# The gate third of adaLN: from PSUM sums beside the output projection to SBUF sums beside the latent projections, with part of the weight split on GpSimd

## The chip, the cores and the metric

The kernel runs on one core of one Trainium2 chip. The metric is the device time of one execution in microseconds (us). The median of three runs before the change is 2997.7 us.

## What is computed

One layer of a latent-token block with D = 4096, 256 latent tokens and 256 context tokens, all in float32. The reference, cut to what matters here:

```python
mod = jax.nn.silu(c) @ w_ada + b_ada                  # (4096) @ (4096, 12288)
shift, scale, gate = jnp.split(mod, 3, axis=-1)
h = modulate(rmsnorm(x, g_norm), shift[:, None], scale[:, None])
proj = h @ w_in                                       # 4096 -> 16384, latent tokens
xa, xb, ga, gb = jnp.split(proj, [LRU_W, MIX_W, MIX_W + LRU_W], axis=-1)
...                                                   # xa also for the context tokens
ya, ya_c = rglru_branch(xa, xa_c, ...)                # two gated linear recurrences, 16 heads
yb = pool_branch(xb, w_pool, b_pool, pool_scale)
mixed = jnp.concatenate([ya * silu(ga), yb * silu(gb)], axis=-1)
x_new = x + gate[:, None] * (mixed @ w_out)           # 8192 -> 4096
return rmsnorm(x_new, g_final)
```

The change is about `gate`, the last third of `mod`: a matrix of 4096 x 4096 multiplied with one vector. It is needed first where the first block of the output projection is finished.

## The kernel before, in words

Tokens lie along the free axis, features along the 128 partitions. Every large weight comes from HBM in tiles of 128 x 1024 float32 (512 KB). A product with such a weight is made in two parts: ScalarE rounds the raw tile to `hi` (L97), another engine subtracts to get `lo = raw - hi` (L99), and TensorE multiplies with both (L566 with `hi`, L567 with `lo`). This is `load_w`. There are 6 buffers for raw tiles, 4 for `hi` and 3 for `lo`. So the `lo` of one weight unit can be written as soon as the unit three places earlier is used up.

The program has three stages on TensorE. First the adaLN columns for shift and scale and the projection `xa`, in nine chunks of the contraction (L237, L337 to L339); here GpSimd makes the `lo` tiles, and VectorE sums adaLN weights into PSUM (`wide`, L213) and finishes each chunk's activations (`hlo`, L131). Then the latent projections: 384 tiles of `w_lat` and 32 of `w_pool`, with the 32 tiles of `w_rec` and the recurrent branch spread among them; here VectorE makes every `lo` tile. Last the output projection, 256 tiles of `w_out`, again with every `lo` on VectorE.

The gate third is cut into four groups of 1024 columns. For each, `gate_units` loads 32 raw tiles, and VectorE adds each, times one element of the vector per partition, to a PSUM accumulator: `accumulate`, L213, with the last step written as two halves `fin` (L219). Two matmuls with a column of ones (L279), a copy and eight small records of transposing matmuls (L192) turn the 1024 sums over partitions into columns of `gate` (L288). Group 0 stands near the end of the latent projections (`GATE_FROM, GATE_END` = 0.9, 0.99 of that list), groups 1 to 3 among the output projection's units (`GATE3`). Its raw tiles share the 6 raw buffers.

The code writes one list of events: `w` units with a weight split, `a` units with a raw tile only, `s` steps. `run` walks it and starts loads a few units ahead. A scheduler of the framework then settles the order of each engine's own queue. Each engine works through its queue in that order. SP's queue issues all the loads.

Of the kernel before, what the change touches and what calls it, by code (L numbers as in the profile page):

```python
# [7 lines left out]
F32 = mybir.dt.float32  # L8
# [3 lines left out]
ADD, SUB, MUL = ALU.add, ALU.subtract, ALU.mult  # L12
# [6 lines left out]
HEADS = 16  # L19
KEEP = 8  # L20
DELAY = 8
GATE3 = (0.08, 0.7)
GATE_FROM, GATE_END = 0.9, 0.99
SPILL_Y = 10
EPS = 1e-6
POOL_ADDS = 3
# [20 lines left out]


def spread(main, side, lo=0.0, hi=1.0):
    """Places the entries of side evenly among those of main, from the fraction lo of main to hi."""  # L50
    out, done, n = [], 0, len(main)
    a, b = lo * n, hi * n
    for i, m in enumerate(main):
        out.append(m)
        want = min(len(side), max(0, int((i + 1 - a) / (b - a) * len(side) + 1e-9)))
        while done < want:
            out.append(side[done])
            done += 1
    return out + side[done:]
# [3 lines left out]
def block_kernel(ctx, tc, xc, cvec, vecs, consts, w_ss, w_gate, w_xa, w_lat, w_pool, w_rec, w_out, out):  # L63
# [7 lines left out]
    rawp = ctx.enter_context(tc.tile_pool(name="raw", bufs=RAWB))  # L71
    hip = ctx.enter_context(tc.tile_pool(name="hi", bufs=HIB))
    lop = ctx.enter_context(tc.tile_pool(name="lo", bufs=LOB))
    ps_mm = ctx.enter_context(tc.tile_pool(name="ps_mm", bufs=4, space=bass.MemoryType.PSUM))
    ps_2 = ctx.enter_context(tc.tile_pool(name="ps_2", bufs=2, space=bass.MemoryType.PSUM))

# [6 lines left out]
    def mm_tile():  # L83
        return ps_mm.tile([P, 512], F32, name="mm", tag="mm")

    def wide_tile():
        return ps_2.tile([P, 1024], F32, name="wide", tag="wide")

    def load_raw(src):
        t = rawp.tile([P, W], F32, name="raw", tag="raw")  # L90
        nc.sync.dma_start(out=t, in_=src)
        return t

    def load_w(src, eng=None):
        raw = load_raw(src)
        hi = hip.tile([P, W], F32R, name="hi", tag="hi")
        act.copy(out=hi, in_=raw)  # L97
        lo = lop.tile([P, W], F32R, name="lo", tag="lo")
        (eng or dve).tensor_tensor(out=lo, in0=raw, in1=hi.bitcast(F32), op=SUB)  # L99
        return hi, lo  # L100

    def run(events):
        queues = {}
        for kind, look in (("w", LOOK), ("a", LOOK_A)):
            queues[kind] = [[e for e in events if e[0] == kind], [], 0, look]
        for e in events:
# [16 lines left out]
    def A_(src, f):  # L123
        return ("a", src, f)

    def S_(f):
        return ("s", f)
# [2 lines left out]
        act.copy(out=hi, in_=src)  # L130
        dve.tensor_tensor(out=lo, in0=src, in1=hi.bitcast(F32), op=SUB)  # L131

# [1 line left out]
    cst = cpool.tile([P, 276], F32, name="cst")  # L134
    nc.sync.dma_start(out=cst, in_=consts)
    ident = cst[:, 0:4]
# [12 lines left out]
    def vrange(name, a, b):  # L149
        o = _VEC[name][0]  # L150
        return vec[:, o + a:o + b]
# [6 lines left out]
    act.activation(out=sig, in_=sig, func=AF.Sqrt)  # L158

    def rstd_of(ps, r, v, s):  # L160
        """Leaves -2 * rsqrt(ps / D + EPS) in r: one Newton step after the square root."""
        dve.tensor_scalar(out=v, in0=ps, scalar1=1.0 / D, scalar2=EPS, op0=MUL, op1=ADD)
        act.activation(out=s, in_=v, func=AF.Sqrt)
        dve.reciprocal(out=r, in_=s)
        dve.tensor_tensor(out=v, in0=v, in1=r, op=MUL)
        dve.tensor_tensor(out=v, in0=v, in1=r, op=MUL)
        dve.scalar_tensor_tensor(out=r, in0=v, scalar=-3.0, in1=r, op0=ADD, op1=MUL)

# [1 line left out]
    colA = cpool.tile([P, KT, 2], F32, name="colA")  # L170
    colB = cpool.tile([P, KT, 2], F32, name="colB")
    gate = cpool.tile([P, KT], F32, name="gate")
# [10 lines left out]
    def take_rows(rows_ps, nv, width):  # L183
        rb = temp("rows")
        act.copy(out=rb[0:nv, :width], in_=rows_ps[0:nv, :width])
        return rb

    def to_cols(rb, nv, width, dst):
        cols = mm_tile()
        nb = width // P  # L190
        for b in range(nb):
            pe.matmul(out=cols[:, nv * b:nv * b + nv], lhsT=rb[0:nv, b * P:(b + 1) * P], rhs=ident[0:nv, 0:nv],  # L192
                      start=True, stop=True)
        dst(cols[:, 0:nv * nb].rearrange("p (b v) -> p b v", v=nv))
# [70 lines left out]
    def gate_units(grp):  # L265
        st = {}

        def unit(k):
            def f(raw):
                if k == 0:  # L270
                    st["accs"] = [wide_tile()]
                    st["fin"] = {}
                accumulate(raw, 0, W, k, st["accs"], 1, 512, st["fin"], k == 0, k == KT - 1)
            return A_(w_gate[grp, k], f)

        def rows():
            r = mm_tile()
            for h in range(2):
                pe.matmul(out=r[0:2, :], lhsT=sel[:, h, 0:2], rhs=st["fin"][h, 0], start=(h == 0), stop=(h == 1))  # L279
            st["rb"] = take_rows(r, 2, 512)  # L280

        def cols():
            o = grp * 8

            def dst(cols):
                g = gate[:, o:o + 8].rearrange("p (h b) -> p b h", h=2)
                bias = vrange("b_ada", 64 + o, 64 + o + 8).rearrange("p (h b) -> p b h", h=2)
                dve.tensor_tensor(out=g, in0=cols, in1=bias, op=ADD)  # L288
            to_cols(st["rb"], 2, 512, dst)
        return [unit(k) for k in range(KT)], S_(rows), S_(cols)  # L290

# [1 line left out]
    hT = [None] * KT  # L293
    hc = [None] * KT

# [20 lines left out]
            hc[k] = None  # L316
        return S_(f)

# [1 line left out]
    acc = [None] * 32  # L320
    xa_sp = [None] * (2 * KEEP) + [dram.tile([P, 512], F32, name=f"xa_sp{o}") for o in range(2 * KEEP, 32)]
    ya_sp = [dram.tile([P, 512], F32, name=f"ya_sp{h}") for h in range(HEADS)]
# [56 lines left out]

    ada = [ada_units(c) for c in range(NC)] + [([],)]  # L380

# [1 line left out]
    xt = []  # L383
    first = ada[0][0] + list(ada[0][1:])

# [50 lines left out]
        if c == 1:  # L436
            events.append(S_(softplus))

# [1 line left out]
    def lru_pieces(h):  # L440
        st = {}

# [94 lines left out]
            return [sigm(d, 0), sigm(d, 1), expo(d), root(d), scan(d, 0), scan(d, 1)]  # L537
        return [conv(0), conv(1)], [gates(0)] + post(0) + [gates(1)], post(1)

# [1 line left out]
    def fold(ps, dst):  # L541
        tmp = temp("fold")
        act.copy(out=tmp[:, 0:T], in_=ps[:, T:T2])
# [118 lines left out]
    events.append(S_(make_pads))  # L662
    events += rec[:2]
    both = spread(main, rec[2:], 0.0, LRU_SPAN / 100)
    gu, gr, gc = gate_units(0)
    both = spread(both, gu, GATE_FROM, GATE_END)
    events += both[:-4] + [gr] + both[-4:-1] + [gc] + both[-1:]

# [1 line left out]
    mix = [None] * 64  # L670

    def make_mix(n):
# [43 lines left out]
    main = [block_units([w_out[blk, i] for i in range(16)], mix, out_evac(blk)) for blk in range(16)]  # L716
    pair = [u for two in zip(main[0], main[1]) for u in two]
    main = spread(pair, [make_mix(n) for n in range(4, 32)], 0.0, 28 / 32) + [u for m in main[2:] for u in m]
    side, held = [], []
    for grp in range(1, 4):  # L720
        gu, gr, gc = gate_units(grp)
        side += gu[:2] + held[:1] + gu[2:4] + held[1:] + gu[4:]
        held = [gr, gc]
    side += held
    events += spread(main, side, GATE3[0], GATE3[1])

    run(events)

# [88 lines left out]
```

## Time and profile before

| | |
|---|---|
| runs | 2989.14, 2997.7, 2999.48 us; median 2997.7 us |
| profiled execution | span 2998.8 us from the first to the last instruction (the page gives no other time of it) |
| TensorE | busy 2909.6 us, 97% of the span |
| VectorE | busy 2256.7 us, 75% |
| ScalarE | busy 1559.9 us, 52% |
| GpSimd | busy 530.7 us, 18% |

The profile names the engines PE (TensorE matmul), PEld (TensorE weight load), DVE (VectorE), ACT (ScalarE), POOL (GpSimd) and SP. L99 is line 99 of the kernel. A busy time is the time in which at least one instruction of the engine was under way. Idle time matters only on the engine that sets the end of a stage.

### The profile page before, as it was taken

Reading aid. Unit: us, or ns where it says so; the run is one execution under the profiler, and the core shown is the slowest. Engines: PE = TensorE matmul, PEld = TensorE weight load, DVE = VectorE, ACT = ScalarE, POOL = GpSimd, SP = SyncE. Lnnn points to the kernel's source line nnn. Section 1 sums busy time; section 2 is a strip of 40 time slices with the busy share of each in tenths; the row PEclk is TensorE's granted clock in tenths of the full one; section 3 lists DMA queues with packets and bytes.
Section 4 is the critical chain, followed back from the end, with each engine's and each line's share of the span. In section 5 each row is a group of like instructions: output and inputs, shape, how many; then the busy total and the mean of one; then the engine's idle time right before and its main releaser. Section 6 shows DMA issues by size and latency. Waiting matters only on the chain.

```text
span 2998.8 us, 40342 instructions
## 1 busy us (share of the span) xinstructions
PE 2909.6 (97%) x14992; PEld 2405.3 (80%) x14992; DVE 2256.7 (75%) x2661; ACT 1559.9 (52%) x2112; POOL 530.7 (18%) x304
## 2 busy tenths in 40 slices
PE   5999999999999999999999999999999999999997
PEld 2656777778788888888888888888888888878886
DVE  6999999998447788888777777778888766665444
ACT  4442344434436666677666666666464443333442
POOL 1466777777520000000000000000000000000000
PEclk9999999999999999999999999999999999999998
DMA  8777787887365555565665566667978888786665
GB/s 301 279 261 252 262 263 261 272 277 250 126 183 176 176 177 175 179 183 172 186 185 181 185 188 189 196 195 251 326 232 318 318 288 286 264 279 216 193 191 171
DMA packets 201142, 679.47 MB, mean 227 GB/s; under 512 B 22000, under 2 KB 30320, under 8 KB 200944
## 3 DMA queue, kind: packets, MB, share of 16 engines
q1 hardware_dynamic: 200944, 676.89, 68.9%
q8 instruction: 117, 1.92, 0.3%
q14 instruction: 81, 0.66, 0.1%
HBM read 661.60 MB, written 15.20 MB: 226 GB/s over the span
## 4 chain that ended last, share of the span: by engine, by line
PE 84%; DVE 6%; DMA 6%; issue 1%; POOL 1%; ACT 1%; SPq 0%; DVEq 0%; POOLq 0%; ACTq 0%
PE mm L566 38%; PE mm L567 19%; PE mm L337 6%; PE mm L338 6%; PE mm L339 6%; DMA raw<-in_w_gate 4%; DVE wide L213 3%; PE wide L478 2%; PE wide L480 2%; PE wide L479 2%; PE mm L237 2%; DMA raw<-in_w_ss 1%; DMA x<-in_xc 1%; DVE lo L99 1%; DVE hlo L131 1%
## 5 line engine op out<-in xcount | busy, mean ns | idle before, releaser
L97 ACT CAST hi<-raw 128x1024 fp32r<-128x1024 f32 x832 | 871.9, 1049 | 968.6 <-PE mm L566 576.3
L99 DVE TENSOR_TENSOR lo<-raw,hi 128x1024 fp32r<-128x1024 f32 x704 | 856.5, 1221 | 371.5 <-PE mm L567 282.7
L566 PE MATMUL mm<-hT,hi 128*128 128x512 f32 x3072 | 1086.8, 399 | 0.0
L567 PE MATMUL mm<-hT,lo 128*128 128x256 f32 x3072 | 862.7, 281 | 0.0
L213 DVE SCALAR_TENSOR_TENSOR wide<-raw,sc,wide 128x1024 f32<-128x1024 f32 (+1 forms) x556 | 662.4, 1240 | 153.5 <-DMA raw<-in_w_gate 119.6
L566 PE MATMUL mm<-mix,hi 128*128 128x512 f32 x2048 | 724.7, 398 | 0.0
L566 PEld LDWEIGHTS mm<-hT,hi 128*128 128x128 f32 x3072 | 577.2, 188 | 144.5 <-ACT mix L130 0.9
L567 PE MATMUL mm<-mix,lo 128*128 128x256 f32 x2048 | 577.4, 282 | 15.3 <-DVE lo L99 15.1
L567 PEld LDWEIGHTS mm<-hT,lo 128*128 128x128 f32 x3072 | 580.2, 189 | 1.3
L566 PEld LDWEIGHTS mm<-mix,hi 128*128 128x128 f32 x2048 | 386.0, 188 | 95.1 <-ACT hi L97 1.7
L337 PE MATMUL mm<-hhi,hi 128*128 128x512 f32 x1024 | 404.1, 396 | 13.1 <-ACT hhi L130 10.7
L338 PE MATMUL mm<-hlo,hi 128*128 128x512 f32 x1024 | 402.1, 393 | 9.0 <-DVE hlo L131 9.0
L567 PEld LDWEIGHTS mm<-mix,lo 128*128 128x128 f32 x2048 | 388.2, 190 | 20.8 <-DVE lo L99 20.5
L339 PE MATMUL mm<-hhi,lo 128*128 128x512 f32 x1024 | 401.0, 392 | 0.0
L99 POOL TENSOR_TENSOR lo<-raw,hi 128x1024 fp32r<-128x1024 f32 x128 | 310.6, 2427 | 207.5 <-PE mm L339 87.8
L337 PEld LDWEIGHTS mm<-hhi,hi 128*128 128x128 f32 x1024 | 193.4, 189 | 73.0 <-ACT hhi L130 11.8
L346 POOL TENSOR_TENSOR acc<-acc,part 128x512 f32<-128x512 f32 x168 | 221.7, 1331 | 116.8 <-ACT part L345 115.8
L338 PEld LDWEIGHTS mm<-hlo,hi 128*128 128x128 f32 x1024 | 193.6, 189 | 53.3 <-DVE hlo L131 13.4
L339 PEld LDWEIGHTS mm<-hhi,lo 128*128 128x128 f32 x1024 | 193.6, 189 | 42.2 <-issue 1.7
L345 ACT COPY part<-mm 128x512 f32<-128x512 f32 x168 | 97.3, 584 | 155.4 <-PE mm L339 155.0
L348 DVE TENSOR_TENSOR acc<-mm,acc 128x512 f32<-128x512 f32 x88 | 60.1, 685 | 56.6 <-PE mm L339 56.5
L478 PE MATMUL wide<-uhi,hi 128*128 128x512 f32 x256 | 100.5, 393 | 0.0
(134 smaller groups left out, 2203.0 us busy)
## 6 DMA issues: line engine op xcount, KB each, us to landing
raw<-in_w_lat SPq DMA_DIRECT2D x384, 512.0 KB, 3.7
raw<-in_w_ss SPq DMA_DIRECT2D x256, 512.0 KB, 4.6
raw<-in_w_out SPq DMA_DIRECT2D x256, 512.0 KB, 4.6
raw<-in_w_xa SPq DMA_DIRECT2D x128, 512.0 KB, 4.4
raw<-in_w_gate SPq DMA_DIRECT2D x128, 512.0 KB, 4.8
raw<-in_w_rec SPq DMA_DIRECT2D x32, 512.0 KB, 3.6
raw<-in_w_pool SPq DMA_DIRECT2D x32, 512.0 KB, 3.7
x<-in_xc SPq DMA_DIRECT2D x32, 256.0 KB, 6.6
```

The source lines that it names most:

```text
L97: act.copy(out=hi, in_=raw)
L99: (eng or dve).tensor_tensor(out=lo, in0=raw, in1=hi.bitcast(F32), op=SUB)
L213: dve.scalar_tensor_tensor(out=accs[v][:, :width], in0=seg, scalar=s, in1=accs[v][:, :width], op0=MUL, op1=ADD)
L337: pe.matmul(out=ps, lhsT=wh, rhs=a, start=(k == 0), stop=False)
L338: pe.matmul(out=ps, lhsT=wh, rhs=b, start=False, stop=False)
L339: pe.matmul(out=ps, lhsT=wl, rhs=a, start=False, stop=(k == n - 1))
L345: act.copy(out=part, in_=ps)
L346: nc.gpsimd.tensor_tensor(out=acc[o], in0=acc[o], in1=part, op=ADD)
L348: dve.tensor_tensor(out=acc[o], in0=ps, in1=acc[o], op=ADD)
L478: pe.matmul(out=o, lhsT=wh[:, g, k, m], rhs=st["hi"][k], start=(k == 0), stop=False)
L566: pe.matmul(out=ps, lhsT=hi[:, k, m], rhs=a, start=first, stop=False)
L567: pe.matmul(out=ps[:, 0:T], lhsT=lo[:, k, m], rhs=a[:, 0:T], start=False, stop=last)
```

## The change

All four groups of the gate third move to the latent projections, spread over the fractions 0.02 to 0.94 of that list. Each weight tile goes to a buffer of a pool of its own (`graw`, two buffers), loaded one ahead. The accumulator is one SBUF tile (`gacc`, one buffer) and no longer a PSUM tile. The sum over partitions is made by eight matmuls that take 128 columns of the accumulator as weights and one column of ones as the moving operand. And of the entries of the latent list every third, where it is a weight unit, gets its `lo` tile from GpSimd: 150 tiles of the 448. The output projection's list holds weights alone. The program is also built with a smaller scratch space for DMA descriptors.

```diff
-GATE3 = (0.08, 0.7)
-GATE_FROM, GATE_END = 0.9, 0.99
+GATE_FROM, GATE_END = 0.02, 0.94
+POOL_LO = 3
+LOOK_G = 1
...
+    graw = ctx.enter_context(tc.tile_pool(name="graw", bufs=1 + LOOK_G))
+    gaccp = ctx.enter_context(tc.tile_pool(name="gacc", bufs=1))
...
+    def load_gate(src):
+        t = graw.tile([P, W], F32, name="graw", tag="graw")
         nc.sync.dma_start(out=t, in_=src)
         return t
...
-        for kind, look in (("w", LOOK), ("a", LOOK_A)):
+        for kind, look in (("w", LOOK), ("a", LOOK_A), ("g", LOOK_G)):
...
-            for kind in ("w", "a"):
+            for kind in ("w", "a", "g"):
...
         def unit(k):
             def f(raw):
+                s = sc6[:, k, 2:3]
                 if k == 0:
-                    st["accs"] = [wide_tile()]
-                    st["fin"] = {}
-                accumulate(raw, 0, W, k, st["accs"], 1, 512, st["fin"], k == 0, k == KT - 1)
-            return A_(w_gate[grp, k], f)
-
-        def rows():
-            r = mm_tile()
-            for h in range(2):
-                pe.matmul(out=r[0:2, :], lhsT=sel[:, h, 0:2], rhs=st["fin"][h, 0], start=(h == 0), stop=(h == 1))
-            st["rb"] = take_rows(r, 2, 512)
+                    st["acc"] = gaccp.tile([P, W], F32, name="gacc", tag="gacc")
+                    dve.tensor_scalar(out=st["acc"], in0=raw, scalar1=s, scalar2=None, op0=MUL)
+                else:
+                    dve.scalar_tensor_tensor(out=st["acc"], in0=raw, scalar=s, in1=st["acc"], op0=MUL, op1=ADD)
+            return ("g", w_gate[grp, k], f)
 
         def cols():
+            c = mm_tile()
+            for b in range(8):
+                pe.matmul(out=c[:, b:b + 1], lhsT=st["acc"][:, b * P:(b + 1) * P], rhs=ones[:, 0:1],
+                          start=True, stop=True)
             o = grp * 8
...
+            dve.tensor_tensor(out=gate[:, o:o + 8], in0=c[:, 0:8], in1=vrange("b_ada", 64 + o, 72 + o), op=ADD)
+        return [unit(k) for k in range(KT)] + [S_(cols)]
...
-    gu, gr, gc = gate_units(0)
-    both = spread(both, gu, GATE_FROM, GATE_END)
-    events += both[:-4] + [gr] + both[-4:-1] + [gc] + both[-1:]
+    gates = [u for grp in range(4) for u in gate_units(grp)]
+    both = [e[:3] + (nc.gpsimd,) if e[0] == "w" and i % POOL_LO == 0 else e for i, e in enumerate(both)]
+    events += spread(both, gates, GATE_FROM, GATE_END)
...
-    for grp in range(1, 4):
-        gu, gr, gc = gate_units(grp)
-        side += gu[:2] + held[:1] + gu[2:4] + held[1:] + gu[4:]
-        held = [gr, gc]
-    side += held
-    events += spread(main, side, GATE3[0], GATE3[1])
+    events += main
...
-    nc = bacc.Bacc("TRN2", target_bir_lowering=False, num_devices=1)
+    nc = bacc.Bacc("TRN2", target_bir_lowering=False, num_devices=1, dynamic_dma_scratch_size=1024)
```

The scheduler decides where the gate steps end up in the queues. They are not spread evenly. A group has one accumulator, which is free again only when the matmuls of the group before have read it. All 32 steps of the first group stand in VectorE's queue ahead of the first `lo` of the latent projections, 20 of them behind the last long run of adaLN sums (`wide`) of the first stage. The other three groups follow each in one crowd. Between the first and the last step of a group stand 41, 36 and 40 weight units, of which GpSimd makes 14, 11 and 13 `lo` tiles. Between the crowds there is no gate step for 59 and 62 units, and none for the last 96.

VectorE's queue in the latent projections of the kernel before, at the convolution of a head (`u`, `ulo`), between two pooling steps:

```order
L459 SCALAR_TENSOR_TENSOR u_11052<-acc_673,vec_85,u_11052 128x2x255
L99 TENSOR_TENSOR lo_10926<-raw_10922,hi_10924 128x1024
L459 SCALAR_TENSOR_TENSOR u_11052<-acc_673,vec_85,u_11052 128x2x255
L459 SCALAR_TENSOR_TENSOR u_11052<-acc_673,vec_85,u_11052 128x2x254
L99 TENSOR_TENSOR lo_10948<-raw_10944,hi_10946 128x1024
L131 TENSOR_TENSOR ulo_11058<-u_11052,uhi_11057 128x512
L99 TENSOR_TENSOR lo_10980<-raw_10976,hi_10978 128x1024
L99 TENSOR_TENSOR lo_11012<-raw_11008,hi_11010 128x1024
```

The same place in the changed kernel, in the second gate group's crowd (`gacc` is the accumulator, `graw` a gate tile):

```order
L462 SCALAR_TENSOR_TENSOR u_11200<-acc_681,vec_91,u_11200 128x2x255
L107 TENSOR_TENSOR lo_11068<-raw_11064,hi_11066 128x1024
L462 SCALAR_TENSOR_TENSOR u_11200<-acc_681,vec_91,u_11200 128x2x255
L283 SCALAR_TENSOR_TENSOR gacc_10183<-graw_12465,sc6_96,gacc_10183 128x1024
L462 SCALAR_TENSOR_TENSOR u_11200<-acc_681,vec_91,u_11200 128x2x254
L283 SCALAR_TENSOR_TENSOR gacc_10183<-graw_12556,sc6_96,gacc_10183 128x1024
L139 TENSOR_TENSOR ulo_11206<-u_11200,uhi_11205 128x512
L107 TENSOR_TENSOR lo_11125<-raw_11121,hi_11123 128x1024
L283 SCALAR_TENSOR_TENSOR gacc_10183<-graw_12663,sc6_96,gacc_10183 128x1024
L283 SCALAR_TENSOR_TENSOR gacc_10183<-graw_12744,sc6_96,gacc_10183 128x1024
L107 TENSOR_TENSOR lo_11179<-raw_11175,hi_11177 128x1024
```

Four gate steps stand among three `lo` tiles; the `lo` tiles that are missing in this list are on GpSimd's queue, one behind the other.

VectorE's queue in the first stage of the kernel before, at the end of the second to last chunk, where the next chunk's columns (`colB`, `colA`) and activations (`hlo`) are made:

```order
L219 SCALAR_TENSOR_TENSOR fin_6070<-raw_6018,sc6_90,wide_5182 128x512
L348 TENSOR_TENSOR acc_884<-mm_6048,acc_884 128x512
L202 TENSOR_TENSOR colB_95<-mm_6117,vec_85 128x8
L203 TENSOR_TENSOR colA_94<-mm_6117,vec_85 128x8
L204 TENSOR_TENSOR colA_94<-colA_94,vec_85 128x8
L131 TENSOR_TENSOR hlo_6129<-x_329,hhi_6128 128x512
L131 TENSOR_TENSOR hlo_6172<-x_334,hhi_6171 128x512
```

The same place in the changed kernel:

```order
L227 SCALAR_TENSOR_TENSOR fin_6074<-raw_6026,sc6_96,wide_5190 128x512
L351 TENSOR_TENSOR acc_892<-mm_6054,acc_892 128x512
L283 SCALAR_TENSOR_TENSOR gacc_7150<-graw_8331,sc6_96,gacc_7150 128x1024
L283 SCALAR_TENSOR_TENSOR gacc_7150<-graw_8439,sc6_96,gacc_7150 128x1024
L283 SCALAR_TENSOR_TENSOR gacc_7150<-graw_8518,sc6_96,gacc_7150 128x1024
L283 SCALAR_TENSOR_TENSOR gacc_7150<-graw_8599,sc6_96,gacc_7150 128x1024
L210 TENSOR_TENSOR colB_101<-mm_6121,vec_91 128x8
L211 TENSOR_TENSOR colA_100<-mm_6121,vec_91 128x8
L212 TENSOR_TENSOR colA_100<-colA_100,vec_91 128x8
L283 SCALAR_TENSOR_TENSOR gacc_7150<-graw_8678,sc6_96,gacc_7150 128x1024
L139 TENSOR_TENSOR hlo_6133<-x_335,hhi_6132 128x512
L283 SCALAR_TENSOR_TENSOR gacc_7150<-graw_8789,sc6_96,gacc_7150 128x1024
```

Steps of the first gate group stand ahead of the columns and between the activations of the last chunk.

## Rows read from the trace of the kernel before

**Rows 1.** The page, part 1: busy us, share and instructions of each engine

```profile
span 2998.8 us, 40342 instructions
...
PE 2909.6 (97%) x14992; PEld 2405.3 (80%) x14992; DVE 2256.7 (75%) x2661; ACT 1559.9 (52%) x2112; POOL 530.7 (18%) x304
```

**Rows 2.** Windows by stage: length, busy us (instructions), clock, DMA share, GB/s

```profile
300.00:870.00 570.00, 561.24 (x2431) 448.49 (x2430) 463.91 (x438) 227.54 (x354) 392.13 (x221) 1.00 0.72 240
870.00:2224.00 1354.00, 1353.98 (x7436) 1164.45 (x7435) 1050.81 (x1418) 900.08 (x1191) 0.00 (x0) 1.00 0.63 197
2224.00:2976.00 752.00, 736.70 (x4132) 632.54 (x4131) 466.88 (x480) 307.28 (x372) 0.00 (x0) 1.00 0.76 253
```

**Rows 3.** Window within the output projection, columns as above

```profile
2433.00:2735.00 302.00, 286.70 (x1585) 243.44 (x1584) 191.47 (x189) 115.98 (x136) 0.00 (x0) 0.99 0.82 275
```

**Rows 4.** Waits of TensorE and VectorE there: us in total, times, longest

```profile
PE mm L567 <- DVE lo L99: 15.1, 13, 2.5
...
DVE wide L213 <- DMA raw<-in_w_gate: 106.9, 62, 5.0
```

**Rows 5.** Timeline of TensorE, group 0's matmuls: start, us, line, count

```profile
2209.66 1.88 PE L279 MATMUL mm<-fin,cst 128*2 128x512 f32 x4
...
2220.14 1.05 PE L192 MATMUL mm<-cst,rows 2*128 2x2 f32 x8
```

**Rows 6.** Groups by line and shape: busy us, mean ns, idle before

```profile
L99 DVE TENSOR_TENSOR lo<-raw,hi 128x1024 fp32r<-128x1024 f32 x704 | 856.5, 1221 | 371.5 <-PE mm L567 282.7 <-issue 45.5 <-ACT hi L97 14.9
...
L213 DVE SCALAR_TENSOR_TENSOR wide<-raw,sc,wide 128x1024 f32<-128x1024 f32 x512 | 632.9, 1282 | 149.0 <-DMA raw<-in_w_gate 119.6 <-DMA raw<-in_w_ss 28.7
...
L566 PEld LDWEIGHTS mm<-mix,hi 128*128 128x128 f32 x2048 | 386.0, 188 | 95.1 <-ACT hi L97 1.7 <-issue 0.9
L99 POOL TENSOR_TENSOR lo<-raw,hi 128x1024 fp32r<-128x1024 f32 x128 | 310.6, 2427 | 207.5 <-PE mm L339 87.8 <-ACT hi L97 54.0 <-POOL acc L346 51.8
...
L348 DVE TENSOR_TENSOR acc<-mm,acc 128x512 f32<-128x512 f32 x88 | 60.1, 685 | 56.6 <-PE mm L339 56.5
...
L131 DVE TENSOR_TENSOR hlo<-x,hhi 128x512 fp32r<-128x512 f32 x32 | 41.8, 1308 | 6.6 <-ACT hhi L130 6.6
...
L131 DVE TENSOR_TENSOR ulo<-u,uhi 128x512 fp32r<-128x512 f32 x32 | 22.7, 710 | 12.3 <-ACT uhi L130 12.2
```

**Rows 7.** Timeline of VectorE, runs of one kind back to back

```profile
753.46 4.86 DVE L213 SCALAR_TENSOR_TENSOR wide<-raw,sc,wide 128x1024 f32<-128x1024 f32 x4 [2.19 <-DMA raw<-in_w_ss]
...
2584.35 3.49 DVE L99 TENSOR_TENSOR lo<-raw,hi 128x1024 fp32r<-128x1024 f32 x3
```

**Rows 8.** Timeline of GpSimd and VectorE at one `hlo`, and a later one

```profile
676.88 2.41 POOL L99 TENSOR_TENSOR lo<-raw,hi 128x1024 fp32r<-128x1024 f32 x1 [0.86 <-POOL acc L346]
...
677.39 2.45 DVE L131 TENSOR_TENSOR hlo<-x,hhi 128x512 fp32r<-128x512 f32 x1
...
787.63 0.69 DVE L131 TENSOR_TENSOR hlo<-x,hhi 128x512 fp32r<-128x512 f32 x1 [2.50 <-ACT hhi L130]
```

**Rows 9.** Windows of the units beside which the three crowds stand

```profile
1210.00:1334.00 124.00, 124.00 (x683) 106.78 (x682) 103.74 (x158) 82.98 (x110) 0.00 (x0) 1.00 0.59 177
1514.00:1626.00 112.00, 112.00 (x615) 96.39 (x614) 83.00 (x105) 72.87 (x93) 0.00 (x0) 1.00 0.60 185
1812.00:1939.00 127.00, 127.00 (x693) 109.14 (x692) 94.06 (x121) 86.31 (x112) 0.00 (x0) 1.00 0.61 193
```

**Rows 10.** Windows of the units before and between them

```profile
870.00:1210.00 340.00, 340.00 (x1865) 292.61 (x1864) 267.72 (x381) 230.36 (x300) 0.00 (x0) 1.00 0.58 177
1334.00:1514.00 180.00, 180.00 (x985) 154.85 (x984) 141.22 (x197) 122.92 (x163) 0.00 (x0) 1.00 0.59 180
1626.00:1812.00 186.00, 186.00 (x1027) 160.31 (x1026) 134.13 (x169) 125.98 (x162) 0.00 (x0) 1.00 0.61 185
```

**Rows 11.** Timeline of VectorE at the end of the second to last chunk

```profile
775.76 0.17 DVE L202 TENSOR_TENSOR colB<-mm,vec 128x8 f32<-128x8 f32 x1 [9.50 <-PE mm L192]
...
779.46 0.69 DVE L131 TENSOR_TENSOR hlo<-x,hhi 128x512 fp32r<-128x512 f32 x1 [2.17 <-ACT hhi L130]
```

More of the change, by code (lines that the diff above doesn't have):

```diff
@@ L92, in load_raw @@
         return t
+    def load_gate(src):
+        t = graw.tile([P, W], F32, name="graw", tag="graw")
+        nc.sync.dma_start(out=t, in_=src)
+        return t
     def load_w(src, eng=None):
@@ L114, in run @@
                     n = q[0][len(q[1])]
-                    q[1].append(load_w(n[1], n[3]) if kind == "w" else load_raw(n[1]))
+                    q[1].append(load_w(n[1], n[3]) if kind == "w" else load_raw(n[1]) if kind == "a" else load_gate(n[1]))
             q = queues[e[0]]
@@ L269, in f @@
             def f(raw):
+                s = sc6[:, k, 2:3]
                 if k == 0:
-                    st["accs"] = [wide_tile()]
-                    st["fin"] = {}
-                accumulate(raw, 0, W, k, st["accs"], 1, 512, st["fin"], k == 0, k == KT - 1)
-            return A_(w_gate[grp, k], f)
-        def rows():
-            r = mm_tile()
-            for h in range(2):
-                pe.matmul(out=r[0:2, :], lhsT=sel[:, h, 0:2], rhs=st["fin"][h, 0], start=(h == 0), stop=(h == 1))
-            st["rb"] = take_rows(r, 2, 512)
+                    st["acc"] = gaccp.tile([P, W], F32, name="gacc", tag="gacc")
[3 more added lines that the diff above has]
+            return ("g", w_gate[grp, k], f)
         def cols():
+            c = mm_tile()
+            for b in range(8):
+                pe.matmul(out=c[:, b:b + 1], lhsT=st["acc"][:, b * P:(b + 1) * P], rhs=ones[:, 0:1],
+                          start=True, stop=True)
             o = grp * 8
[L285 to L290, printed above, removed]
+            dve.tensor_tensor(out=gate[:, o:o + 8], in0=c[:, 0:8], in1=vrange("b_ada", 64 + o, 72 + o), op=ADD)
+        return [unit(k) for k in range(KT)] + [S_(cols)]
     hT = [None] * KT
@@ L718, in block_kernel @@
     main = spread(pair, [make_mix(n) for n in range(4, 32)], 0.0, 28 / 32) + [u for m in main[2:] for u in m]
-    side, held = [], []
-    for grp in range(1, 4):
-        gu, gr, gc = gate_units(grp)
-        side += gu[:2] + held[:1] + gu[2:4] + held[1:] + gu[4:]
-        held = [gr, gc]
-    side += held
-    events += spread(main, side, GATE3[0], GATE3[1])
+    events += main
     run(events)
```

## Prediction

> **What bounds the kernel now.** I read the page first: TensorE is busy 2909.6 us of 2998.8 [rows 1], so only about 89 us are there to be won at all, and any engine that falls behind TensorE costs time at once. Then the windows by stage [rows 2]. In the latent projections (870 to 2224 us) TensorE is busy for all of 1354 us at full clock: nothing can be gained there, only lost. VectorE is busy 1051 of 1354 us and GpSimd not at all. In the output projection (2224 to 2976) TensorE is busy 736.7 of 752. The gap of 15.3 lies between 2433 and 2735, where the gate groups 1 to 3 are summed [rows 3], and the waits say why [rows 4]: TensorE waits 15.1 us for `lo` tiles on VectorE, which itself waits 106.9 us for gate tiles from HBM, with `lo` work queued behind. The clock of that window is 0.99, another 3 us.
>
> **What the change takes away.** With no gate step left there, the output projection gets back 15.3 us of waits and 3 us of clock. On TensorE the matmuls for the gate columns go: 1.88 + 1.05 = 2.93 us for a group [rows 5], 11.7 for four.
>
> **What TensorE gets instead.** Eight matmuls a group with 128x128 weights and one moving column. The rows of the old ones show that a float32 matmul leaves two records, so 16 a group. Bounds: 1.05/8 = 0.13 us a record as in the small transposing matmuls [rows 5], or 0.188 us, a load of 128x128 weights [rows 6]. That is 2.1 to 3.0 us a group, 8.4 to 12 in all. I take 12, since the weights have that shape. Matmuls out and in cancel. The gain is then 15.3 + 3 + 11.7 - 12 = 18 us, at most 22.
>
> **What VectorE and GpSimd get.** A VectorE instruction overlaps the next, so I price by runs: four gate sums of this size take 4.86 us, 1.20 a step; a `lo` adds (3.49 - 1.22)/2 = 1.14 [rows 6, 7]. A gate step that reads its accumulator from SBUF rather than PSUM isn't in the trace; I keep 1.20. On GpSimd a `lo` takes 2.43 us instead of 1.22 [rows 6].
>
> The question is whether the two engines can work at the same time. The trace answers it. GpSimd starts a `lo` at 676.88 and ends at 679.29. VectorE's `hlo`, which reads two SBUF tensors, starts at 677.39 and lasts 2.45 us, to 0.55 behind GpSimd's end; with GpSimd idle it takes 0.69 [rows 8]. In the mean it takes 1308 ns in the first stage, while the same shape (`ulo`) takes 710 in the latent projections without GpSimd [rows 6]. Instructions with an operand in PSUM don't show this: `acc` 685 ns, the gate sums 1282 [rows 6]. So a VectorE instruction with two SBUF inputs waits out a GpSimd `lo`. Gate steps had been immune, and with the accumulator in SBUF they are not.
>
> The Trainium skill ("Perfetto Trace Analysis", Optimizing Scalar/DVE Operations) says of work moved from VectorE to GpSimd that "offloading operations between those two might not help", as they share a read port. By that rule each microsecond of a GpSimd `lo` is one that VectorE loses; a reading by busy shares alone (a third of the `lo` work leaves VectorE) would have the crowds below free of charge and the time near 2984. The `hlo` row agrees with the rule.
>
> **The crowds.** The order shows gate groups 1 to 3 as crowds of 32 steps. I set the demand against the same units in the trace of before [rows 9]: VectorE's busy time there, less 1.14 for each `lo` that went to GpSimd, plus 32 x 1.20 = 38.4, plus 2.41 (the single GpSimd row) for each GpSimd `lo`.
> - First crowd, 124 us: 103.7 - 14 x 1.14 + 38.4 = 126.1 on VectorE; with GpSimd's 33.7 it is 159.8, 36 too much.
> - Second, 112 us: 83.0 - 12.5 + 38.4 = 108.9; with 26.5 it is 135.4, 23 too much.
> - Third, 127 us: 94.1 - 14.8 + 38.4 = 117.7; with 31.3 it is 149.0, 22 too much.
>
> Upper bound 81 us. If the engines didn't exclude each other only the first would exceed, by 2: lower bound 0. Two things soften the upper bound. The three `lo` buffers give a lead of two units. A unit takes 124/41 = 3.0 us, so 6 us for each crowd, 18. And 42 of VectorE's instructions there read one SBUF operand or PSUM (`fold` sums, the bias step of `yb`) and can run beside GpSimd: at some 0.35 us 15. I take 81 - 18 - 15 = 48. Behind a late `lo` on VectorE stand the recurrent branch's and the pooling's steps; on TensorE every later unit waits, and nothing gives the time back, since it had no idle time in this stage.
>
> **Between the crowds** [rows 10], with 37, 19 and 19 `lo` tiles on GpSimd: 267.7 - 42.2 + 89.2 = 314.7 of 340 us; 141.2 - 21.7 + 45.8 = 165.3 of 180; 134.1 - 21.7 + 45.8 = 158.2 of 186. That fits on average, with 85% to 93% taken. A burst of pooling and scan steps may exceed the lead. I take 6 us, from 0 to 30.
>
> **The first stage.** The 32 steps of group 0 need 38 us, and up to 2.43 us more each when they meet GpSimd, 116 together. VectorE has 570 - 464 = 106 us idle there [rows 2], most of it in the last chunk, where most of these steps stand. What counts is the turn from the second to last chunk to the last: VectorE is idle 9.50 us ahead of `colB` and 2.17 ahead of the first `hlo` [rows 11], and now four gate steps stand ahead of the first and one ahead of each `hlo` behind. `colB` still fits, an `hlo` may come 1 to 3 us later. With single steps at earlier turns and two gate loads ahead of the first weights (1 MB, about 4 us at the 240 to 250 GB/s of the stages [rows 2]) I take 8 us, from 0 to 25.
>
> **The sum.** 2998.8 + 48 + 6 + 8 - 18 = 2998.8 + 44 = 3043 us. The profiled execution is 1.1 us above the median of the runs.
>
> **Rivals.**
> 1. The crowds cost nothing: 2984, or 2977 with the cheap column matmuls and no loss in the first stage. GpSimd would do its `lo` tiles while VectorE waits for something anyway. For it: VectorE alone nearly fits each crowd (126 of 124, 109 of 112, 118 of 127). Against it: over 22 us would have to hide in each crowd. It decides when less than about 5 us of TensorE waits stand in each.
> 2. Half of it: crowds 22, between 2, first stage 5, so 2998.8 + 29 - 18 = 3010. For it: the leads may recover within a crowd, where the steps don't stand evenly.
> 3. GpSimd's `lo` tiles come late everywhere: while VectorE runs back to back, each waits for one or two of its instructions (1.2 us each), then takes 2.4, against a lead of 6 us. At 0.5 us for each of the 112 outside the crowds that is 56 us in place of 6: 3093. Against it: in the first stage GpSimd's mean of 2427 ns is hardly above the 2.41 of the single row, so it seldom waits long there; but VectorE runs fewer two-input steps there.
>
> **Chances.** Forecast 0.57 (its own range 3016 to 3080), rival 1 0.13, rival 2 0.15, rival 3 0.15. About 0.5% (15 us) is what a measurement of this kernel tells from no change: below 2983 is most of rival 1, so faster 0.10; rival 2 and the rest of rival 1 are the same, 0.18; slower 0.72. The range takes in both signs, from the middle of rival 1 to rival 3: 2980 to 3095.
>
> **What would show it.** In the profile after: TensorE waits for `lo` in the latent projections, about 15 to 25 us in each crowd and few between; the latent stage some 54 us longer; the output projection about 27 us shorter without waits; VectorE's `lo`, gate and scan steps with a mean well above 1.2 us or 0.7 us where GpSimd runs; 32 gate steps before the latent stage with a few microseconds lost at the chunk turns. Wrong would be a latent stage that still takes 1354 us plus the column matmuls, or a loss spread evenly over all GpSimd tiles, or VectorE in the crowds waiting mainly for gate tiles from HBM rather than for GpSimd.

## The result and the profile after

The changed kernel takes 3095.3 us (median of 4 runs, 3079.5 to 3101.0) against 2995.5 for the kernel before (2989.1 to 2999.5): a ratio of 1.0322, interval 1.0299 to 1.0345. It is slower, as forecast, but by about 100 us where 44 were forecast, and just beyond the upper end of the stated range, 3095. The page of the changed kernel, as in [rows 1]:

```profile
span 3094.8 us, 40543 instructions
PE 2933.6 (95%) x15008; PEld 2423.4 (78%) x15008; DVE 2303.4 (74%) x2507; ACT 1549.7 (50%) x2108; POOL 958.6 (31%) x454
```

The windows by stage of the changed kernel, as in [rows 2], with the stages' new bounds:

```profile
300.00:892.00 592.00, 569.33 (x2439) 452.49 (x2438) 519.85 (x471) 229.38 (x358) 405.24 (x223) 0.99 0.77 260
892.00:2348.00 1456.00, 1385.59 (x7491) 1185.12 (x7490) 1150.53 (x1339) 891.90 (x1189) 417.16 (x149) 0.98 0.64 205
2348.00:3072.00 724.00, 724.00 (x4096) 628.05 (x4095) 357.85 (x373) 306.35 (x369) 0.00 (x0) 1.00 0.64 194
```

From first to last matmul the first stage takes 826.6 us (803.7 before, +23), the latent projections 1455.5 (1354.3, +101) and the output projection 724.1 (752.2, -28). The sum is +96, the difference of the spans. The output projection did what was forecast: no wait, full clock, no gate work. The latent stage took all of that back, and more than three times as much.

The changed kernel's waits of TensorE in the latent stage, where there were none before:

```profile
PE mm L570 <- DVE lo L107: 47.2, 28, 4.2
PE wide L483 <- DVE lo L107: 12.5, 7, 4.2
PE mm L570 <- POOL lo L107: 6.6, 3, 5.9
PE mm L569 <- DVE yb L551: 3.9, 1, 3.9
```

They add up to 70.2 us, about the stage's 1456.0 less TensorE's 1385.6. Nearly all is for `lo` tiles of VectorE; GpSimd's own tiles cost 6.6, of which 5.9 is the last tile of the stage (below). TensorE's busy time grows by the other 31.6 us. All four groups' column matmuls stand in this stage, with 7.4 us; of the old ones only group 0's did, with 2.9 [rows 5]. The changed kernel's windows of the three crowds, with the stretch right behind the first as the second row, show where the time goes:

```profile
1243.00:1395.00 152.00, 132.94 (x683) 112.11 (x682) 146.56 (x171) 80.13 (x108) 45.47 (x15) 0.94 0.74 248
1395.00:1458.00 63.00, 56.98 (x294) 47.86 (x293) 57.79 (x75) 35.19 (x46) 16.93 (x7) 0.95 0.53 170
1586.00:1718.00 132.00, 118.75 (x621) 100.19 (x620) 116.52 (x119) 71.44 (x92) 32.81 (x12) 0.96 0.79 267
1909.00:2056.00 147.00, 132.77 (x687) 111.72 (x687) 131.61 (x132) 82.46 (x108) 39.10 (x14) 0.97 0.79 269
```

Unit by unit against the kernel before, the crowds lost 27.9, 19.0 and 21 us and the units right behind them 9.1, 3.6 and 2: 82.6 together. Ahead of the first crowd 10.8 us went, in the rest about 8. VectorE is busy 146.6 us of the first crowd's 152, and that is with time in it in which its instructions were shut out. The changed kernel's timeline of VectorE and GpSimd shows such a place in that crowd (rows of the other engines are left out):

```profile
1342.49 0.42 DVE L551 TENSOR_TENSOR yb<-mm,fold 128x256 f32<-128x256 f32 x1
...
1342.83 1.28 DVE L283 SCALAR_TENSOR_TENSOR gacc<-graw,sc,gacc 128x1024 f32<-128x1024 f32 x1
...
1342.97 3.39 POOL L107 TENSOR_TENSOR lo<-raw,hi 128x1024 fp32r<-128x1024 f32 x1 [8.87 <-PE mm L570]
...
1344.02 2.50 DVE L620 TENSOR_SCALAR yb<-yb,vec 128x256 f32<-128x256 f32 x1
...
1346.89 0.41 DVE L620 TENSOR_SCALAR yb<-yb,vec 128x256 f32<-128x256 f32 x1
```

GpSimd starts its `lo` at 1342.97, while a gate step runs to 1344.11, and ends at 1346.36. It takes 3.39 us where the single row of [rows 8] had 2.41: about one more microsecond, the rest of that gate step. Then VectorE's bias step of `yb`, which takes 0.41 us when it stands alone (1346.89), takes 2.50 and ends 0.16 behind GpSimd. They take turns, in both directions. The turns are not always one for one. The last GpSimd tile of the stage, and the longest entry of VectorE's timeline beside it:

```profile
2331.85 11.38 POOL L107 TENSOR_TENSOR lo<-raw,hi 128x1024 fp32r<-128x1024 f32 x1 [5.03 <-PE mm L570]
...
2332.31 4.44 DVE L139 TENSOR_TENSOR mix<-yb,mix 128x256 fp32r<-128x256 f32 x13
```

VectorE ran `mix` and `lo` instructions, each with two SBUF inputs, without a pause from 2331.18 to 2341.03. GpSimd's tile ended 2.2 us behind the last of them, so it seems to have waited for the whole run. TensorE waited 5.9 us for it.

The changed kernel's groups by line and shape show the turns in the means:

```profile
L283 DVE SCALAR_TENSOR_TENSOR gacc<-graw,sc,gacc 128x1024 f32<-128x1024 f32 x124 | 192.1, 1549 | 39.7 <-DMA graw<-in_w_gate 39.1
...
L289 PE MATMUL mm<-ones,gacc 128*128 128x1 f32 x64 | 7.4, 245 | 0.0
```

And its groups in the latent stage alone:

```profile
L107 POOL TENSOR_TENSOR lo<-raw,hi 128x1024 fp32r<-128x1024 f32 x149 | 417.2, 2800 | 1041.8 <-PE mm L570 554.4 <-ACT hi L105 224.1 <-PE wide L483 65.6
...
L551 DVE TENSOR_TENSOR gv<-mm,fold 128x256 f32<-128x256 f32 x63 | 26.3, 417 | 28.7 <-ACT fold L546 28.7
L620 DVE TENSOR_SCALAR yb<-yb,vec 128x256 f32<-128x256 f32 x32 | 24.8, 797 | 0.2
```

A GpSimd `lo` takes 2800 ns (2427 in the first stage before [rows 6]), and a gate step 1549, where steps of its size that summed in PSUM took 1282 [rows 6]. The bias step of `yb` went from 409 to 797. `gv`, with an operand in PSUM, stays as it was (420 before).

The last view of the changed kernel is VectorE's timeline in the first stage, at the turn to the last chunk, where `fin` began at 759.69 and `colB` at 775.76 before [rows 11]:

```profile
772.42 0.68 DVE L351 TENSOR_TENSOR acc<-mm,acc 128x512 f32<-128x512 f32 x1
776.16 1.29 DVE L283 SCALAR_TENSOR_TENSOR gacc<-graw,sc,gacc 128x1024 f32<-128x1024 f32 x1 [3.06 <-DMA graw<-in_w_gate]
778.70 1.28 DVE L283 SCALAR_TENSOR_TENSOR gacc<-graw,sc,gacc 128x1024 f32<-128x1024 f32 x1 [1.26 <-DMA graw<-in_w_gate]
779.91 2.72 DVE L227 SCALAR_TENSOR_TENSOR fin<-raw,sc,wide 128x512 f32<-128x512 f32 x4
...
789.62 4.62 DVE L283 SCALAR_TENSOR_TENSOR gacc<-graw,sc,gacc 128x1024 f32<-128x1024 f32 x2 [3.64 <-DMA graw<-in_w_gate]
794.17 0.15 DVE L210 TENSOR_TENSOR colB<-mm,vec 128x8 f32<-128x8 f32 x1
```

`fin` and `colB` are each some 20 us late. Ahead of them VectorE stands still for gate tiles from HBM (3.06, 1.26 and 3.64 us) and two gate steps take 4.62 us. By the units, 6 us were lost before 700 us, 10.9 at this turn and 5.7 in the last chunk.

### The profile page after: what moved, and what is told of

Its sections match the earlier page's. It is cut to its first block, busy times and chain, and to the rows that moved or that the text cites. A ratio compares the mean times of both kernels' runs of the same rounds, so it can differ in the third digit from the quotient of the medians.

```text
span 3094.8 us, 40543 instructions
## 1 busy us (share of the span) xinstructions
PE 2933.6 (95%) x15008; PEld 2423.4 (78%) x15008; DVE 2303.4 (74%) x2507; ACT 1549.7 (50%) x2108; POOL 958.6 (31%) x454
## 4 chain that ended last, share of the span: by engine, by line
PE 66%; DVE 19%; DMA 7%; issue 4%; ACT 2%; POOL 1%; POOLq 0%; SPq 0%; DVEq 0%; ACTq 0%
PE mm L569 32%; PE mm L570 16%; PE mm L340 4%; PE mm L341 4%; PE mm L342 4%; DVE lo L107 3%; DVE wide L221 3%; DVE gacc L283 3%; DMA graw<-in_w_gate 3%; DMA raw<-in_w_ss 3%; PE wide L483 1%; PE wide L481 1%; PE wide L482 1%; DMA x<-in_xc 1%; PE mm L245 1%
## 5 line engine op out<-in xcount | busy, mean ns | idle before, releaser
L107 POOL TENSOR_TENSOR lo<-raw,hi 128x1024 fp32r<-128x1024 f32 x278 | 734.7, 2643 | 1253.6 <-PE mm L570 554.4
L107 DVE TENSOR_TENSOR lo<-raw,hi 128x1024 fp32r<-128x1024 f32 x554 | 697.0, 1259 | 494.7 <-PE mm L570 410.6
L570 PEld LDWEIGHTS mm<-hT,lo 128*128 128x128 f32 x3072 | 586.7, 191 | 60.2 <-DVE lo L107 50.2
L221 DVE SCALAR_TENSOR_TENSOR wide<-raw,sc,wide 128x1024 f32<-128x1024 f32 (+1 forms) x436 | 508.4, 1226 | 23.5 <-DMA raw<-in_w_ss 23.1
L283 DVE SCALAR_TENSOR_TENSOR gacc<-graw,sc,gacc 128x1024 f32<-128x1024 f32 x124 | 192.1, 1549 | 39.7 <-DMA graw<-in_w_gate 39.1
L483 PE MATMUL wide<-uhi,lo 128*128 128x512 f32 x256 | 102.6, 401 | 12.5 <-DVE lo L107 12.5
```

The source lines that it names most:

```text
L221: dve.scalar_tensor_tensor(out=accs[v][:, :width], in0=seg, scalar=s, in1=accs[v][:, :width], op0=MUL, op1=ADD)
L283: dve.scalar_tensor_tensor(out=st["acc"], in0=raw, scalar=s, in1=st["acc"], op0=MUL, op1=ADD)
L483: pe.matmul(out=o, lhsT=wl[:, g, k, m], rhs=st["hi"][k], start=False, stop=(k == 1))
L570: pe.matmul(out=ps[:, 0:T], lhsT=lo[:, k, m], rhs=a[:, 0:T], start=False, stop=last)
```

## The experiments

Three theories. **A**: VectorE and GpSimd take turns at SBUF, so their work adds up, and TensorE waits where the sum is too much. **B**: GpSimd's own `lo` tiles come late (rival 3). **C**: the crowds of gate steps and their loads alone do it, GpSimd's part doesn't matter. Each kernel was run beside the kernel before: 2996.6 us (13 runs) for the first four, 2997.7 (10 runs) for the others.

**e1: the change without GpSimd's `lo` tiles in the latent stage.**

```diff
-    both = [e[:3] + (nc.gpsimd,) if e[0] == "w" and i % POOL_LO == 0 else e for i, e in enumerate(both)]
```

> The changed kernel, with every lo tile of the latent projections back on VectorE; gate groups still in crowds. Theory A (VectorE and GpSimd take turns at SBUF, so their work adds up): VectorE's demand in the three crowds becomes 103.7 + 38.4 = 142 of 124 us, 121 of 112 and 132 of 127, 33 us too much in all in place of 81; the latent stage lasts about 1400 us (before 1354, changed 1456), the first stage keeps its 23 us, the output projection its gain of 28: about 3030 us in all, 3015 to 3045. Theory B (the GpSimd lo tiles come late, and TensorE waits for those): without them the latent stage is at 1360 to 1370 and the whole at 2995 to 3005. Theory C (the crowds alone, or their loads from HBM, hold VectorE up; GpSimd does no harm): no better than the changed kernel, 3085 to 3100, since VectorE has more to do.

2998.2 us, ratio 1.0005 (0.9993 to 1.0017). The window of e1's latent stage:

```profile
892.00:2261.00 1369.00, 1359.89 (x7485) 1170.76 (x7484) 1109.74 (x1478) 895.60 (x1184) 0.00 (x0) 1.00 0.69 218
```

TensorE's waits in it:

```profile
PE mm L569 <- ACT i L495: 6.1, 1, 6.1
PE mm L570 <- DVE lo L107: 2.4, 4, 1.4
```

Crowds alone cost that stage 15 us, 4.5 of them column matmuls, and TensorE waits 2.4 us for VectorE and 6.1 for ScalarE: C is out for the latent stage. The first stage loses 23.4 us all the same (counted from the span's start): there C is right. A's time was too high: it had about 1400 us for the latent stage, which took 1369, and 14 us more is in the output projection (709.9 us against 724.1, see the last section). The numbers that came are B's, 1360 to 1370 and 2995 to 3005. So this run shows that most of the latent stage's loss needs GpSimd's tiles, but doesn't tell A from B; TensorE's waits above and e5 do.

**e2: the kernel before with every third `lo` on GpSimd.** The gate work is untouched.

```diff
+    both = [e[:3] + (nc.gpsimd,) if e[0] == "w" and i % 3 == 0 else e for i, e in enumerate(both)]
```

> The kernel before, with the 150 lo tiles of the latent projections on GpSimd and the gate third where it was. Theory A: no stretch asks for more than 85% to 96% of TensorE's time, so the latent stage grows by 10 to 25 us only (the changed kernel lost about 16 us outside its crowds): 3005 to 3025 us. Theory B: a late tile costs what it cost in the changed kernel, some 0.5 to 0.7 us for each of 150: 3070 to 3100. Theory C: no change, 2990 to 3000.

3038.8 us, ratio 1.0145 (1.0124 to 1.0166): between A and B, neither's number. The latent stage takes 45 us more, by its window:

```profile
869.00:2268.00 1399.00, 1366.13 (x7436) 1168.87 (x7435) 1069.62 (x1273) 893.06 (x1193) 396.52 (x149) 1.00 0.61 190
```

TensorE's waits in it are again for VectorE:

```profile
PE mm L567 <- DVE lo L99: 20.7, 19, 2.8
PE wide L480 <- DVE lo L99: 4.9, 3, 2.1
PE mm L567 <- POOL lo L99: 4.3, 3, 3.0
```

VectorE has 149 tiles less to make and is busy longer, 1069.6 us against 1050.8 [rows 2]. Most of the loss comes in two stretches, set unit by unit against the kernel before: 19 us between 1175 and 1400 us, and 17 behind 2100, where the crowd of gate group 0 stands.

**e3: the change with the gate steps spread evenly.** A small VectorE instruction makes each step's scalar out of the newest `hi` tile (times 0), so that the scheduler can't draw the step forward. GpSimd's tiles stay.

```diff
-                s = sc6[:, k, 2:3]
+                s = pinp.tile([P, 1], F32, name="pin", tag="pin")
+                dve.scalar_tensor_tensor(out=s, in0=cur["hi"].bitcast(F32)[:, 0:1], scalar=0.0, in1=sc6[:, k, 2:3],
+                                         op0=MUL, op1=ADD)
```

> The changed kernel, with each gate step tied to the weight unit beside which the event list has it: its scalar is first copied by a small VectorE instruction that also reads one column of that unit's hi tile (times zero). So no step can run ahead, the 128 steps stand evenly, and none in the first stage. Theory A: the first stage is back at 804 us. In the latent projections both engines' work now adds up to 359 of 340 us, 328 of 304, 297 of 298 and about 307 of 307 in four parts: some 45 us too much, and 10 for clock dips; the output projection keeps its gain: about 3020 us, 3005 to 3040. Theory C: crowds gone, the latent stage within 10 us of before: 2970 to 2985. Theory B: as the changed kernel less the first stage's loss: 3060 to 3080.

3047.3 us, ratio 1.0174 (1.0144 to 1.0204): a little above A's range. The first stage loses 3.2 us instead of 23. The latent stage still loses 81, and not evenly: 27 and 32 us in the parts that took 340 and 304 us before, for which theory A's sums were 359 and 328, and 12 and 10 in the other two, whose time its sums just filled. The window of the units that took 340 us before [rows 10]:

```profile
873.00:1240.00 367.00, 347.63 (x1881) 296.66 (x1880) 324.67 (x407) 227.13 (x300) 105.10 (x37) 0.99 0.67 210
```

TensorE's waits in e3's latent stage, VectorE's and GpSimd's:

```profile
PE mm L577 <- DVE lo L108: 40.0, 27, 4.1
PE mm L577 <- POOL lo L108: 6.8, 3, 5.9
```

And the group of the small instructions, the pins:

```profile
L284 DVE SCALAR_TENSOR_TENSOR pin<-hi,sc 128x1 f32<-128x1 f32 x128 | 58.7, 459 | 21.8 <-ACT hi L106 21.6
```

Part of the loss is the experiment's own: the pins have two SBUF inputs and are shut out too, 459 ns each, and 151 in the next kernel. For 128 that is 39 us of VectorE's time.

**e4: e3 without GpSimd's tiles.** Both edits above together.

> Both together: gate steps tied to their units, every lo tile on VectorE. Theory A: VectorE alone needs 312 of 340 us, 287 of 304 and less later, so the latent stage grows by the column matmuls and a few us (5 to 15), the first stage is as before, the output projection keeps its gain of 28: 2972 to 2985 us, faster than before by 0.4% to 0.8%. Theory C gives the same, theory B too: the run tells how much of the loss is neither, and whether there is a version better than both.

2958.1 us, ratio 0.9877 (0.9862 to 0.9892): faster than both kernels, and than expected. The windows of its latent stage and output projection:

```profile
874.00:2229.00 1355.00, 1354.89 (x7490) 1169.33 (x7489) 1157.86 (x1642) 899.98 (x1188) 0.00 (x0) 1.00 0.74 233
2229.00:2939.00 710.00, 710.00 (x4098) 620.93 (x4097) 360.01 (x382) 307.06 (x371) 0.00 (x0) 1.00 0.66 198
```

All 128 gate steps and all `lo` tiles on VectorE, and TensorE is busy for the whole latent stage. By stages, counted from the span's start: +4.6, +0.4 and -42.3 us. Of the last, 28 are what the change also won there; the other 14 are the last section's.

**e5: e4 with idle GpSimd work that reads SBUF.** Two GpSimd multiplies of a scratch tile of zeros at each gate step. The pins take their factor 0 from that tile, so the next gate step's pin reads the result, and nothing else.

```diff
+                for _ in range(2):
+                    nc.gpsimd.tensor_tensor(out=cur["scr"][:, 0:512], in0=cur["scr"][:, 0:512], in1=cur["scr"][:, 0:512], op=MUL)
```

> The kernel with even gate steps and all lo tiles on VectorE (2958 us), and beside each of the 128 gate steps two extra GpSimd instructions of 128x512 (about 1.33 us each, 340 us in all) that multiply an SBUF scratch tile of zeros with itself. No engine waits for their results, save the small scalar copy of the next gate step, some three units later. Theory A (turns at SBUF): VectorE is busy 1158 us of the latent stage's 1355, and 340 more don't fit: 100 to 145 us more, 3060 to 3105, with TensorE waiting for lo tiles of VectorE. Theory B (GpSimd's own lo tiles are late): no lo tile is on GpSimd, so 2955 to 2965.

3075.9 us (2 runs), ratio 1.0262 (1.0242 to 1.0283): A's range. The window of the latent stage:

```profile
874.00:2345.00 1471.00, 1385.53 (x7489) 1179.12 (x7488) 1362.57 (x1648) 894.03 (x1196) 394.47 (x256) 0.99 0.69 214
```

Waits in it, TensorE's and VectorE's:

```profile
PE mm L581 <- DVE lo L109: 65.8, 62, 4.0
...
DVE pin L286 <- POOL scr L289: 0.9, 1, 0.9
```

And its groups:

```profile
L109 DVE TENSOR_TENSOR lo<-raw,hi 128x1024 fp32r<-128x1024 f32 x448 | 617.9, 1386 | 57.5 <-PE mm L581 44.6 <-ACT hi L107 4.0 <-issue 3.7
...
L289 POOL TENSOR_TENSOR scr<-scr 128x512 f32<-128x512 f32 x256 | 394.5, 1541 | 968.2 <-DVE pin L286 958.2
L294 DVE SCALAR_TENSOR_TENSOR gacc<-graw,pin,gacc 128x1024 f32<-128x1024 f32 x124 | 253.5, 2044 | 2.5
```

GpSimd makes nothing that TensorE uses, the pins wait 0.9 us for it in all, and the latent stage is 116 us longer than in e4. A gate step takes 2044 ns in place of 1281. B can't explain this: there is no `lo` tile of GpSimd's to come late.

**e6: the same with GpSimd work that only writes.**

```diff
+                for _ in range(4):
+                    nc.gpsimd.memset(cur["scr"][:, 0:704], 0.0)
```

> The same, but the extra GpSimd instructions are four memsets of 128x704 for each gate step (about 0.7 us each, 350 us in all): they write SBUF and read nothing. If what shuts VectorE out is GpSimd's reading (the Trainium skill, SBUF State Buffer, Who interferes with whom, says that two-input VectorE instructions meet only GpSimd instructions that read): 2955 to 2970 us. If any GpSimd work at SBUF shuts it out: as the run with reads, 3060 to 3105. If GpSimd has nothing to do with it: 2958.

2956.9 us (2 runs), ratio 0.9865 (0.9846 to 0.9885): no loss against e4, with GpSimd nearly as busy as in e5. The window of the latent stage:

```profile
874.00:2229.00 1355.00, 1354.94 (x7491) 1169.68 (x7491) 1165.29 (x1649) 902.82 (x1196) 352.13 (x512) 1.00 0.73 233
```

And its groups:

```profile
L109 DVE TENSOR_TENSOR lo<-raw,hi 128x1024 fp32r<-128x1024 f32 x448 | 545.7, 1218 | 134.2 <-PE mm L581 81.5 <-issue 27.3 <-ACT hi L107 10.9
...
L294 DVE SCALAR_TENSOR_TENSOR gacc<-graw,pin,gacc 128x1024 f32<-128x1024 f32 x124 | 158.8, 1281 | 2.5
```

So it is GpSimd's reading of SBUF, not its being busy, that stops VectorE: gate steps 1281 ns here, 2044 there. The Trainium skill ("SBUF — State Buffer", Who interferes with whom) says that a VectorE instruction with two SBUF inputs contends with a GpSimd instruction that reads SBUF and not with one that only writes it; e5 and e6 agree, with 116 us and none.

**e7: e3 with half as many tiles on GpSimd (75 in place of 149).**

```diff
-POOL_LO = 3
+POOL_LO = 6
```

> Even gate steps, with every sixth entry's lo tile on GpSimd (76 tiles) in place of every third (150, 3047 us) or none (2958 us). Theory A: VectorE's 1158 us, less 76 x 1.14, plus 76 x 2.41, is 1254 of 1355: it fits on average, and bursts cost 15 to 35 us: 2973 to 2993. Theory B (a fixed price for each late tile, 89 us for 150): 45 us, 3003.

2990.2 us, ratio 0.9968 (0.9956 to 0.9980): in A's range, but not for A's reason alone. The window of the latent stage:

```profile
873.00:2244.00 1371.00, 1359.08 (x7488) 1170.28 (x7487) 1182.34 (x1567) 893.95 (x1187) 203.46 (x75) 1.00 0.72 229
```

It loses 16 us against e4, and the output projection 14 more, without a tile of GpSimd's in it.

**e8: e4 with one matmul behind a recurrent unit issued as two halves**, at 25 of the 32 recurrent units, to change TensorE's rhythm (last section).

```diff
+                        if cur.pop("cut", False) and not first:
+                            pe.matmul(out=ps[:, T:T2], lhsT=hi[:, k, m], rhs=a[:, T:T2], start=False, stop=False)
+                            pe.matmul(out=ps[:, 0:T], lhsT=hi[:, k, m], rhs=a[:, 0:T], start=False, stop=False)
```

> The kernel with even gate steps and all lo tiles on VectorE (2958 us), with one difference: the first hi matmul behind each unit of the recurrent weights is issued as two halves of 256 columns. In the traces TensorE runs the pairs of matmuls at one of two steady rhythms, 0.353 us or 0.347 us a pair; it falls back to the slow one at each recurrent unit, and column matmuls or a stall can bring the fast one, which then lasts. If the split issue brings the fast rhythm too, 416 units of eight pairs save up to 22 us: 2936 to 2948 us. If the rhythm is set by something else: 2956 to 2964.

2961.2 us, ratio 0.9881 (0.9865 to 0.9898): the same as e4. The rhythm in the trace didn't change: the split doesn't bring the fast one, and what sets it is something else.

## Why the prediction came out short

**The mechanism holds.** VectorE's two-input instructions and GpSimd's `lo` tiles exclude each other, as the one `hlo` row had suggested [rows 8]; e5 shows it with GpSimd work that TensorE never needs. (The mean of 710 ns for `ulo` is of the whole run; in the latent stage alone it is 686.) The Trainium skill's sentence that moving work between the two "might not help" ("Perfetto Trace Analysis", Optimizing Scalar/DVE Operations) holds too, and is mild: in e2 the move of 149 tiles cost 45 us.

**The crowds: the step that failed.** The prediction had an upper bound of 36 + 23 + 22 = 81 us and took off 18 for the lead and 15 for VectorE's instructions with one SBUF operand or one in PSUM, which left 48. Measured with the units right behind: 37, 22.6 and 23, in all 82.6. Neither deduction showed in the time:
- The 15 us. Of the 42 instructions 34 are `fold` sums with an operand in PSUM. GpSimd doesn't hold them up, but by the starts and ends of their records they stood beside a GpSimd `lo` for only 1.6 us in the three crowds. That they can share the time doesn't mean that they do. The other 8, the bias steps of `yb`, are shut out as well: 797 ns in the mean of the stage, 409 before.
- The 18 us. Ahead of the first crowd the lead was spent: the units there had lost 10.8 us, and TensorE waited once more at 1233 us. Ahead of the second TensorE had run 128 us without a wait, so its lead can't have been spent there. But in the second and third crowd VectorE stood idle for gate tiles from HBM, time that the sum had counted as room. VectorE's waits in the windows 1586 to 1718 and 1909 to 2056:

```profile
DVE gacc L283 <- DMA graw<-in_w_gate: 14.3, 8, 2.9
...
DVE gacc L283 <- DMA graw<-in_w_gate: 12.1, 9, 3.3
```

The prediction named these waits as a sign of being wrong, if they were the main thing. By themselves they aren't: e1 has 17.3 us of them in its latent stage and loses 15 there in all. How much of the 18 us they took wasn't measured apart.

That the sum came out at the bound is partly luck. Put VectorE's work and GpSimd's as one sum for the latent stage: VectorE's busy time without GpSimd tiles (e1 for the change, e4 for the pinned kernels, [rows 2] for e2), less 1.14 for each tile given away, plus 2.41 for each tile on GpSimd. For e5 it is 256 multiplies at 1.33 us, as GpSimd's sums of that shape took in the kernel before; the 394 us measured have waits in them. Against it the stage's loss over its 1354 us:

| kernel | sum, us | of 1354 | loss, us |
|---|---|---|---|
| e4 even gates, no GpSimd tile | 1158 | 86% | 0 |
| e1 crowds, no GpSimd tile | 1110 | 82% | 15 |
| e2 GpSimd tiles, no gates moved | 1240 | 92% | 45 |
| e7 even gates, 75 tiles | 1253 | 93% | 17 |
| the change | 1299 | 96% | 101 |
| e3 even gates, 149 tiles | 1347 | 99% | 81 |
| e5 even gates, 340 us of idle reads | 1498 | 111% | 117 |

No sum over the stage would have given these losses: at 92% a good part is lost already, and at 111% less than the excess of 144. GpSimd's tiles alone cost 45 us and the crowds alone 15, the two together 101, so 41 exist only in the company of the other. That TensorE has a two-unit lead, and that VectorE in a burst also waits for ScalarE in its queue, fits this; how much each adds wasn't measured apart.

**Between the crowds** 6 us were taken within 0 to 30; the stage lost 18.6 outside the crowds, 4.5 of it by the column matmuls, which had a term of their own, and 5.9 by the one late tile at the end. Priced at 12, these measure 7.4 for four groups, in the 64 records that were counted on.

**The clock** of the latent stage wasn't priced. By the PEclk column the four windows above were at the 1.2 GHz level for twice the missing share: 152 x 0.12 + 63 x 0.10 + 132 x 0.08 + 147 x 0.06 = 44 us. They are windows in which TensorE waited, and the same stage without waits was at full clock [rows 2]. It explains most of the growth of TensorE's busy time (44 / 2 = 22 of 31.6 us). What it cost by itself stays open, since in a stretch that waits for VectorE a faster TensorE would only wait longer.

**The first stage: "`colB` still fits" failed.** 8 us were taken, 23 measured. The step looked at `colB` and `hlo`; but `fin`, whose sums the columns are made of, was 20 us late already, with gate steps ahead of it. The step counted the gate steps' time and left out that VectorE's queue, in order, also waits for their tiles (8 us in the rows shown). e1 has the same loss (23.4) without GpSimd tiles in the next stage, and with the steps tied to the latent stage it is 3.2 (e3) and 4.6 (e4).

**The output projection** was right: -27 forecast, -28.1 measured. That it is so close is partly luck: the changed kernel ran it in the slower of two rhythms, which nothing in the prediction chose, and e4 has -42.3 (last section). Rival 1 (the crowds cost nothing) and rival 2 (half) are refuted; rival 3 gives about the measured time, 3093, but by a mechanism that cost 6.6 us here, and e5 loses more with no tile of GpSimd's that could come late: it is VectorE's `lo` tiles that TensorE waits for. Rival 1's 2984 doesn't follow from its terms: without the 48 and the 6 the sum is 2998.8 + 8 - 18 = 2989. With 82.6 for 48, 18.6 for 6 and 23 for 8 the sum is 2998.8 + 124 - 28 = 3095.

## What to carry to other kernels

Before giving VectorE's work to GpSimd, add GpSimd's time to VectorE's, for all that reads SBUF, and ask whether the busiest stretches, not the mean, still have room for it. The good half of this change was the other one: work moved off a stage with waits into a stage whose VectorE was at 78%, with each step tied to its place; with that alone (e4) the kernel is 1.2% faster, 14 us of it by the rhythm below. And in an in-order queue a moved step brings the wait for its load along: count what stands behind it until the tile lands.

## What the runs showed of the hardware

TensorE runs the same stream of matmul pairs (512 and 256 columns) at one of two speeds, at full granted clock and without a wait. The output projection's 2048 pairs take 724 us in the changed kernel and 710 in e4, both windows with TensorE busy throughout and PEclk 1.00: 0.3535 us a pair against 0.3466. In e1, e3, e4, e5, e6 and e8 it was the faster one, in the changed kernel and e7 the slower. So some 14 us of the differences between these profiled executions have nothing to do with the engines' work; which rhythm the other executions had isn't known. A recurrent unit often ends the fast rhythm in the latent stage, and a stall or the column matmuls were often ahead of its start. What sets it stays open: the one try to set it, e8, changed nothing.
